# Weight sums of a hybrid encoder step: no declared VectorE time, 256 KB transfers, loaded 8 steps ahead and stored 3 behind

## The chip, the cores and the metric

The kernel runs on one core of a Trainium2 chip. The metric is the device time of one launch in microseconds. Five engines work side by side and are synchronised by semaphores: TensorE (PE; its weight loads are the row PEld), VectorE (DVE), ScalarE (ACT), GpSimd (POOL) and SyncE (SP), which issues most of the DMA transfers in the order of its queue.

## What is computed

One layer of an encoder, for a prompt of 2048 rows and for a decode batch of 8 sequences with 16 rows each, which share the weights. All is float32.

```python
h   = rms_norm(x, norm_g[0]);  z = h @ w_in          # one projection, 3592 columns
att = chunk-band attention(qa, ka, va)               # 8 heads x 64, own chunk of 64 and 8 before it
hb  = mLSTM(qb, kb, vb, ib, fb)                      # 4 heads x 128, chunked recurrence
mix = concat(rms_norm(att), sigmoid(ob) * headnorm(hb)) @ w_out
x   = x + rms_norm(mix, norm_g[1])
u   = rms_norm(x, norm_g[2]) @ w_up                  # 1024 -> 5632
y   = causal depthwise conv of width 3 over u
f   = (gelu(gate) * up) @ w_down                     # 2816 -> 1024
x   = x + rms_norm(f, norm_g[3])
```

Outputs are both groups' x, the keys and values, the mLSTM states and the convolution's tails.

## The kernel before

**Products.** Every float32 operand is split into a rounded high part (ScalarE) and a remainder (VectorE), and a product is three TensorE matmuls (`mm3`, lines 95 to 97). The FFN's two products use a scheme of seven half-size products in place of eight, which needs sums and differences of weight blocks besides the blocks themselves.

**Stages.** In the first stage `w_in` is worked through in 14 groups of columns, for each of two halves of the rows (`seq`, 28 groups): `va` and `vo` groups give rows (`group_rows`, two steps for each tile of 128 rows: 18 in the first half, 16 in the second), `qk` and `qb` groups give columns (`group_T`, 12 steps). The next group's weights are loaded and split meanwhile (`load_group`, half a group at a time). Then `project` (line 964) makes `mix @ w_out` for 17 tiles, and the FFN follows in three blocks of rows.

**Pipes and pace.** Attention and mLSTM are cut into small steps that are put between the group products. Two pipes (`Pipe`) hold them: `att_stream` takes heads from a queue as their `qk` group is done, `mem_stream` takes mLSTM heads. Each step yields what it declares: TensorE us and VectorE us. The same is yielded by every group step and by the work that rides along with it: the weight split, the norms and the weight sums. `pump(pe, dve)` (line 173) adds them up in `clock` and then steps the pipes while VectorE's clock is behind `SHARE` = 0.615 of TensorE's, with at most two tries, one for each pipe in turn; at the end it forgets what VectorE's clock is behind by more than 4.0:

```python
for _ in range(2):
    if clock[1] >= SHARE * clock[0]:
        break
    turn[0] ^= 1
    c = pipes[turn[0]].step()
    ...
clock[1] = max(clock[1], SHARE * clock[0] - (0.0 if idle == 2 else 4.0))
```

Nothing in this pace measures the chip: it sets the order of the program alone. A compile-time scheduler then places the instructions on each engine, mostly in that order; the loads that are wrapped in `keep_in_program_order` keep theirs.

**The drain.** `project` loads tiles two ahead. When it comes to tile 8 (line 970), whose rows need the second half's attention, it runs both pipes empty (`drain`, line 960) and opens the FFN's memory over that of the first stage (`open_ffn`, line 1039). From there on the pipes hold the FFN's norm and transposes (`h2_units`; x2r is loaded at line 1069, scaled at 1081, transposed at 1089).

**A step of attention.** `load_head` loads a head's query, key and value blocks (lines 339 and after). `att_unit` makes scores (lines 384, 385), adds the bias and takes the row minimum on VectorE (line 395), exponentiates on ScalarE (396), transposes (67), splits (407, 408), multiplies with the values (420, 421) and adds the halves (427). After a pair of heads the block is scaled (438, `attst`) and stored to `mixd` (442). For 640 keys the unit declares 0.533 and 0.667 us, then 0.535 and 0.667, and every second unit 1.2 and 0.34 more; a head load declares 0, about 1.8 and then 0.34 to 0.68, the scaling 0.43 and 0.7.

**The weight sums.** `weight_sums` (line 1175) makes the blocks that the seven-product scheme needs: 22 blocks of `w_up` and 11 of `w_down`, each of 128 x 2048 float32 (1 MB), seen as four pieces of 128 x 512. A block is loaded with one transfer (L1185) to the tile `wsum` (one buffer), four steps go by, four VectorE additions or subtractions (L1189) overwrite the pieces in the order of `up` or `down` in four more steps, and one transfer stores the block (L1191) to `wsd` or `wtd` in device memory. That makes 11 steps a block, 363 in all, one for each group step from the second group on (line 1251). Each addition declares 0.69 us of VectorE. The FFN stage reads `wsd` and `wtd` again as 256 KB pieces (`wu<-wsd`, `wdr<-wtd`).

Of the kernel before, what the change touches and what calls it, by code (L numbers as in the profile page):

```python
# [3 lines left out]

# [6 lines left out]
F32 = mybir.dt.float32  # L11
# [6 lines left out]
P = 128  # L18
# [26 lines left out]
def hymba_step(ctx: ExitStack, tc: tile.TileContext, I: dict, O: dict):  # L45
    nc = tc.nc
# [7 lines left out]
    def ps_mm(name):  # L54
        return psum.tile([P, 512], F32, tag="mm", name=name)

    def ps_big(name):
        return psum.tile([P, 1024], F32, tag="big", name=name)

    def ps_sm(name):  # L60
        return psum.tile([P, 512], F32, tag="sm", name=name)
# [66 lines left out]
    pr = p1.enter_context(tc.tile_pool(name="pr", bufs=1))  # L128
# [920 lines left out]
    def quad(name):  # L1049
        return ffn.p3.tile([P, 512], F32, tag="q", name=name, bufs=11)  # L1050
# [124 lines left out]
    def weight_sums():  # L1175


        add, sub = ALU.add, ALU.subtract
        up = ((2, 3, 2, add), (3, 0, 3, sub), (0, 2, 0, sub), (1, 1, 0, sub))
        down = ((0, 1, 0, sub), (1, 2, 1, sub), (2, 2, 0, sub), (3, 3, 2, sub))  # L1180
        todo = [(I["w_up"][f], wsd[f], up, f"u{f}") for f in range(NF)]
        todo += [(I["w_down"][i], wtd[i], down, f"d{i}") for i in range(NF // 2)]
        for src, dst, plan, nm in todo:
            t = pr.tile([P, 4, 512], F32, tag="wsum", name=f"wsum{nm}", bufs=1)
            tc.keep_in_program_order(nc.sync.dma_start(t, src.rearrange("p (a n) -> p a n", a=4)))  # L1185
            for _ in range(4):
                yield 0.0, 0.0
            for o, x, y, op in plan:
                nc.vector.tensor_tensor(t[:, o, :], t[:, x, :], t[:, y, :], op=op)  # L1189
                yield 0.0, 0.69  # L1190
            nc.sync.dma_start(dst.rearrange("p (a n) -> p a n", a=4), t)  # L1191
            for _ in range(3):
                yield 0.0, 0.0

    def norm_steps(half):

# [16 lines left out]
    next(norms)  # L1213
    load_bias()
    sums = weight_sums()
    for n_, (half, gi) in enumerate(seq):
        wh, wl, _ = pend
# [5 lines left out]
        i = int(g[2])  # L1223
        nm = f"{g}_{half}"
# [129 lines left out]
    def evacuate(b, j, acc, dh):  # L1354

        t = FBLOCKS[b][j]
        half = half_row(j, dh, f"fr{t}_{dh}")
        ssq = p3.tile([P, 1], F32, tag=f"dssq{j}", name=f"dssq{t}_{dh}", bufs=2)
        if b < len(FBLOCKS) - 1 or dh == 0:
            nc.vector.tensor_copy(half, acc)  # L1360
            acc = half
        nc.scalar.activation(junk, acc, AF.Square, accum_out=ssq)
        return half, acc, ssq
# [58 lines left out]
    for b, tiles in enumerate(FBLOCKS):  # L1422
        last = b == len(FBLOCKS) - 1
        nt = len(tiles)
        n = HALF[b]
# [96 lines left out]
        for f in range(NF):  # L1522
# [5 lines left out]
            nm = f"{b}_{f}"  # L1528
            a, d_, ec = ps_mm(f"ua{nm}"), ps_sm(f"ub{nm}"), ps_big(f"uec{nm}")
            e, c = ec[:, 0:512], ec[:, 512:1024]  # L1530
# [75 lines left out]
        if not last:  # L1606
# [4 lines left out]
            for q in range(42):  # L1611
                p, u = divmod(q, 6)
# [24 lines left out]
                for j in range(3):  # L1637
# [4 lines left out]
                    elif p == D2:  # L1642
                        o = quad(f"c11_{b}_{j}")
# [7 lines left out]
                    elif p == D4:  # L1651
                        o = quad(f"c21_{b}_{j}")
# [9 lines left out]
        for dh in range(2):  # L1662
# [50 lines left out]
            for j in range(nt):  # L1713
                half, _, ssq = evacuate(b, j, accs[j], dh)
# [98 lines left out]
```

## Time and profile before

| | us |
|---|---|
| median of 3 runs | 2854.73 (2854.33 to 2854.81) |
| the profiled execution | 2856.95 |
| its span, first to last instruction | 2855.2 |
| PE busy | 2722.0 |
| DVE busy | 1973.3 |
| mean granted TensorE clock | 0.986 |

The profile is one execution of the program. Busy times are those of each engine's instructions; a matmul's end is modelled, so a full PE is not PE at its peak. A row of a group gives the line, engine, operation, what is written and read, the count, and busy and mean times. In rows of waits, the instruction named first stood idle until the one behind the arrow was done. "SPq" rows are DMA issues on SP's queue; the rows of DMA issues give the size of one and the median time from issue to landing. The granted clock (PEclk) is the share of full TensorE speed. By the stretches of the span, the first stage lasts until about 1035 us, the output projection until about 1440, the FFN from there to the end.

### The profile page before, as it was taken

How to read it: one execution, taken by the hardware profiler on the slowest of the kernel's cores; microseconds unless marked ns; L12 is line 12 of the kernel's file. 1: busy time of each engine (PE TensorE's matmuls, PEld its weight loads, DVE VectorE, ACT ScalarE, POOL GpSimd, SP SyncE). 2: the span in 40 equal slices, each digit the busy share in tenths (PEclk: the TensorE clock that was granted, in tenths of full speed). 3: DMA queues.
4: the chain of work that ended last, by engine and by line, in shares of the span. 5: the costliest groups of instructions: out<-in, count | busy, mean ns of one | idle time of the engine just before them, and what ended most of it. 6: DMA issues, size and time to landing. Idle time of an engine off the chain costs nothing.

```text
span 2855.2 us, 47306 instructions
## 1 busy us (share of the span) xinstructions
PE 2722.0 (95%) x16389; PEld 2538.4 (89%) x16389; DVE 1973.3 (69%) x3640; ACT 1437.2 (50%) x2908; POOL 436.3 (15%) x876
## 2 busy tenths in 40 slices
PE   7899999989999999988999999999999999999998
PEld 7899998888889997876899998889999878999887
DVE  5355456666646667765688888858888885888855
ACT  4345444634436565463455555754545665555543
POOL 1000001111100003302411110011111121222221
PEclk9999999999999999998999999999999999999999
DMA  6654458578776665434665556765555797555586
GB/s 232 218 177 145 143 192 275 171 261 276 265 235 206 220 194 171 126 91 145 215 195 178 168 176 202 263 226 157 175 176 168 247 335 236 177 176 178 176 293 203
DMA packets 342831, 575.47 MB, mean 202 GB/s; under 512 B 57442, under 2 KB 173630, under 8 KB 334014
## 3 DMA queue, kind: packets, MB, share of 16 engines
q1 hardware_dynamic: 303998, 538.61, 58.8%
q10 hardware_dynamic: 38592, 33.83, 3.6%
q8 instruction: 129, 2.11, 0.3%
q14 instruction: 112, 0.92, 0.1%
HBM read 424.24 MB, written 151.21 MB: 202 GB/s over the span
## 4 chain that ended last, share of the span: by engine, by line
PE 51%; DMA 3%; DVE 3%; issue 2%; ACT 1%; POOL 1%; SPq 0%; DVEq 0%; POOLq 0%; ACTq 0%
PE uec L95 6%; PE uec L96 6%; PE uec L97 6%; PE ua L97 3%; PE ua L96 3%; PE ua L95 3%; PE dn L97 3%; PE dn L95 3%; PE dn L96 3%; PE dnm L97 2%; PE dnm L95 2%; PE dnm L96 2%; PE ub L96 1%; PE ub L97 1%; PE ub L95 1%
## 5 line engine op out<-in xcount | busy, mean ns | idle before, releaser
L95 PE MATMUL uec<-B,wuh 128*128 128x384 f32 (+1 forms) x720 | 234.3, 327 | 1.5 <-DVE uu L1438 1.5
L96 PE MATMUL uec<-B,wuh 128*128 128x384 f32 (+1 forms) x720 | 235.2, 327 | 0.0
L97 PE MATMUL uec<-B,wul 128*128 128x384 f32 (+1 forms) x720 | 234.2, 327 | 0.0
L1285 ACT CAST wuh<-wu 128x512 fp32r<-128x512 f32 x315 | 172.9, 617 | 81.5 <-PE uec L96 79.9
L1286 DVE TENSOR_TENSOR wul<-wu,wuh 128x512 fp32r<-128x512 f32 x315 | 202.7, 684 | 2.9 <-DMA x2d<-mx 2.9
L95 PE MATMUL dn<-wdh,gh 128*128 128x512 f32 x422 | 167.3, 396 | 11.7 <-ACT gh L1285 8.7
L96 PE MATMUL dn<-wdl,gh 128*128 128x512 f32 x422 | 167.8, 398 | 0.0
L97 PE MATMUL dn<-wdh,gl 128*128 128x512 f32 x422 | 163.5, 401 | 1.4 <-DVE gl L1286 1.4
L95 PE MATMUL vo<-wi_h,hT 128*128 128x256 f32 x544 | 156.6, 288 | 0.0
L96 PE MATMUL vo<-wi_l,hT 128*128 128x256 f32 x544 | 155.3, 286 | 0.0
L97 PE MATMUL vo<-wi_h,hT 128*128 128x256 f32 x544 | 155.2, 285 | 0.0
L1286 DVE TENSOR_TENSOR wdl<-wdr,wdh 128x512 fp32r<-128x512 f32 x198 | 127.4, 690 | 28.5 <-ACT wdh L1285 25.2
L396 ACT ACTIVATE tmp<-tmp,mn 128x640 f32<-128x640 f32 (+4 forms) x128 | 97.7, 764 | 80.6 <-DVE mn L395 73.1
L1285 ACT CAST wdh<-wdr 128x512 fp32r<-128x512 f32 x198 | 112.1, 618 | 50.1 <-DMA wdr<-in_w_down 21.6
L95 PEld LDWEIGHTS uec<-B,wuh 128*128 128x128 f32 x720 | 135.0, 188 | 2.7 <-DVE uu L1438 2.5
L96 PEld LDWEIGHTS uec<-B,wuh 128*128 128x128 f32 x720 | 135.2, 188 | 0.1
L97 PEld LDWEIGHTS uec<-B,wul 128*128 128x128 f32 x720 | 135.1, 188 | 0.0
L395 DVE CUSTOM_DVE_ANT_0 tmp<-s,nb 128x640 f32<-128x640 f32 (+4 forms) x128 | 94.0, 735 | 56.2 <-PE s L385 51.6
L95 PE MATMUL qk<-hT,wi_h 128*128 128x384 f32 (+1 forms) x384 | 129.0, 336 | 1.5 <-ACT qk_st L228 0.9
L96 PE MATMUL qk<-hT,wi_h 128*128 128x384 f32 (+1 forms) x384 | 129.0, 336 | 0.0
L97 PE MATMUL qk<-hT,wi_l 128*128 128x384 f32 (+1 forms) x384 | 128.9, 336 | 0.0
L95 PE MATMUL qb<-hT,wi_h 128*128 128x384 f32 (+1 forms) x384 | 127.9, 333 | 0.5 <-ACT qb_st L226 0.5
(428 smaller groups left out, 8898.0 us busy)
## 6 DMA issues: line engine op xcount, KB each, us to landing
wu<-wsd SPq DMA_DIRECT2D x264, 256.0 KB, 3.6
wu<-in_w_up SPq DMA_DIRECT2D x198, 256.0 KB, 3.8
wdr<-in_w_down SPq DMA_DIRECT2D x110, 256.0 KB, 5.7
wi_raw<-in_w_in SPq DMA_DIRECT2D x52, 512.0 KB, 4.8
gq<-gsd SPq DMA_DIRECT2D x62, 384.0 KB, 5.0
wsumu<-in_w_up SPq DMA_DIRECT2D x22, 1024.0 KB, 7.1
wsd<-wsumu SPq DMA_DIRECT2D x22, 1024.0 KB, 5.5
wdr<-wtd SPq DMA_DIRECT2D x88, 256.0 KB, 5.6
```

The source lines that it names most:

```text
L95: nc.tensor.matmul(out, ah, bh, start=start, stop=False, skip_group_check=onto)
L96: nc.tensor.matmul(out, ah, bl, start=False, stop=False, skip_group_check=onto)
L97: nc.tensor.matmul(out, al, bh, start=False, stop=stop, skip_group_check=onto)
L395: nc.vector.tensor_tensor_reduce(o_, s_, b_, 1.0, 3e38, ALU.add, ALU.min, accum_out=mn)
L396: nc.scalar.activation(tmp[:, :n], tmp[:, :n], AF.Exp, bias=mn, scale=-1.0, accum_out=rsum[:, i % 4, hh:hh + 1])
L1285: nc.scalar.copy(h, r)
L1286: nc.vector.tensor_tensor(l, r, h, op=ALU.subtract)
```

## The change

Each block is now four tiles of 128 x 512 (tags `wsum0` to `wsum3`, two buffers each, so 16 KB instead of 8 KB of each partition). A table `acts` gives what is done at which step. With n the block's number: piece i is loaded at step 11n + i, addition e is made at step 11n + 11 + e, and the piece that it wrote is stored at step 11n + 14 + e. So the first addition comes eight steps after the last piece's load, and each store three steps after its addition. Within one step the earlier block's actions come first. The loads keep their place in the program order, as before. All steps yield 0.0, 0.0, the additions too. There are still 132 additions of 128 x 512, and a block still takes 11 steps; the last store is at step 369. The 33 loads and 33 stores of 1 MB become 132 loads and 132 stores of 256 KB, whose rows of 2 KB lie 8 KB apart in device memory.

```diff
-from collections import deque
+from collections import defaultdict, deque
...
         todo += [(I["w_down"][i], wtd[i], down, f"d{i}") for i in range(NF // 2)]
-        for src, dst, plan, nm in todo:
-            t = pr.tile([P, 4, 512], F32, tag="wsum", name=f"wsum{nm}", bufs=1)
-            tc.keep_in_program_order(nc.sync.dma_start(t, src.rearrange("p (a n) -> p a n", a=4)))
-            for _ in range(4):
-                yield 0.0, 0.0
-            for o, x, y, op in plan:
-                nc.vector.tensor_tensor(t[:, o, :], t[:, x, :], t[:, y, :], op=op)
-                yield 0.0, 0.69
-            nc.sync.dma_start(dst.rearrange("p (a n) -> p a n", a=4), t)
-            for _ in range(3):
-                yield 0.0, 0.0
+        acts = defaultdict(list)
+        for n, (src, dst, plan, nm) in enumerate(todo):
+            t = []
+
+            def load(i, src=src, t=t, nm=nm):
+                t.append(pr.tile([P, 512], F32, tag=f"wsum{i}", name=f"wsum{nm}_{i}", bufs=2))
+                tc.keep_in_program_order(nc.sync.dma_start(t[i], src[:, i * 512:(i + 1) * 512]))
+
+            def combine(e, plan=plan, t=t):
+                o, x, y, op = plan[e]
+                nc.vector.tensor_tensor(t[o], t[x], t[y], op=op)
+
+            def store(e, dst=dst, plan=plan, t=t):
+                o = plan[e][0]
+                nc.sync.dma_start(dst[:, o * 512:(o + 1) * 512], t[o])
+
+            for i in range(4):
+                acts[11 * n + i].append(lambda i=i, f=load: f(i))
+                acts[11 * n + 11 + i].append(lambda i=i, f=combine: f(i))
+                acts[11 * n + 14 + i].append(lambda i=i, f=store: f(i))
+        for step in range(max(acts) + 1):
+            for act in acts[step]:
+                act()
+            yield 0.0, 0.0
```

## The prediction

> **What bounds the kernel now.** I read the page first, then the busy time by stretch, then instructions and waits of the stretches where TensorE is not full.
>
> ```profile
> span 2855.2 us, 47306 instructions
> ...
> PE 2722.0 (95%) x16389; PEld 2538.4 (89%) x16389; DVE 1973.3 (69%) x3640; ACT 1437.2 (50%) x2908; POOL 436.3 (15%) x876
> ```
>
> TensorE is the bound: 133 us of the span are not covered by its matmuls, and no change outside TensorE can win more than that, plus what slow clock costs. So the question is where those 133 us lie and which of them the weight sums can reach. By stretch (the first columns after the length are busy us and instruction counts of PE, PEld, DVE, ACT and POOL, then granted clock, DMA share, GB/s):
>
> ```profile
> core 0: us, PE busy (x) PEld busy (x) DVE busy (x) ACT busy (x) POOL busy (x), PEclk, DMA share, GB/s
> 206.00:386.00 180.00, 180.00 (x1295) 179.16 (x1294) 86.57 (x185) 87.86 (x199) 1.70 (x11) 1.00 0.45 138
> 386.00:505.00 119.00, 108.67 (x742) 102.46 (x741) 75.50 (x193) 55.74 (x149) 14.09 (x39) 1.00 0.83 265
> ...
> 600.00:710.00 110.00, 102.60 (x701) 97.67 (x700) 62.11 (x178) 43.13 (x118) 16.55 (x47) 0.98 0.82 274
> 710.00:826.00 116.00, 106.12 (x653) 96.79 (x652) 64.89 (x174) 45.25 (x113) 19.80 (x45) 0.96 0.74 245
> 826.00:1035.00 209.00, 205.77 (x1560) 202.62 (x1560) 125.55 (x291) 112.93 (x284) 11.94 (x38) 1.00 0.70 222
> ...
> 1240.00:1296.00 56.00, 42.52 (x257) 35.50 (x255) 35.15 (x72) 33.85 (x69) 0.73 (x2) 0.88 0.21 58
> 1296.00:1308.00 12.00, 11.99 (x53) 9.14 (x52) 3.00 (x5) 1.10 (x3) 0.19 (x1) 1.00 0.44 100
> 1308.00:1328.00 20.00, 7.76 (x33) 6.59 (x34) 14.16 (x12) 8.36 (x16) 12.38 (x14) 0.60 0.54 187
> ```
>
> Two stretches stand out. From 1240 to 1296 TensorE idles 13.48 us and runs at a clock of 0.88; from 1308 to 1328 it idles 12.24 us at 0.60. The first is the drain: `load(8)` (line 970) empties both pipes before the FFN's memory is opened, and whatever attention is left runs alone, with no product between its steps:
>
> ```profile
> L395 DVE CUSTOM_DVE_ANT_0 tmp<-s,nb x16: 814/824/825, 1239.4 to 1287.5; 128x640 f32<-128x640 f32 x16
> ```
>
> So 16 score units are left over. The second hole is its echo:
>
> ```profile
> 1302.43 0.69 DVE L438 TENSOR_TENSOR attst<-ao,rinv 128x512 f32<-128x512 f32 x1 [4.79 <-PE ao L67]
> ...
> 1303.15 0.55 SPq L442 DMA_DIRECT2D mixd<-attst  x1
> ...
> 1304.41 0.94 SPq L1069 DMA_DIRECT2D x2r<-x2d  x2
> ...
> 1313.71 1.11 PE L1089 MATMUL h2T_pt<-ident,x2r 128*128 128x128 f32 x4 [5.72 <-DVE x2r L1081]
> ...
> 1318.67 1.97 PE L67 MATMUL mT_pt<-ident,mr 128*128 128x128 f32 x8 [0.71 <-DVE mr L987]
> 1325.26 1.97 PE L67 MATMUL mT_pt<-ident,mr 128*128 128x128 f32 x8 [4.62 <-DVE mr L987]
> ```
>
> SP issues in order: the store of the last attention block waits for L438, and behind it stand the loads of x2r that the first FFN transposes need. They go out at 1304.41 and the transpose starts 9.3 us later.
>
> **Part 1: the sums declare no time.** Each `pump` steps the pipes until declared VectorE time reaches 0.615 of declared TensorE time, at most two tries, one for each pipe. A block of sums now declares 4 x 0.69 us over its 11 steps. The second half's groups take 16 (row groups) or 12 (column groups) steps. 33 blocks are 363 steps; the first half uses 5 x 18 + 8 x 12 = 186, so 177 fall in the second half: 177 x 4/11 x 0.69 = 44.4 us of declared VectorE time that will go to attention and mLSTM steps instead. What does the drain need? From the costs in the code, a pair of 640-column units declares 3.01 us VectorE and 3.34 us TensorE, net of the share 3.01 - 0.615 x 3.34 = 0.96; eight pairs 7.7. Three head loads at about 2.1 make 6.4, closings (0.70 - 0.615 x 0.43 = 0.44) 1.5: together about 16 us. Attention is tried once a pump, so in the groups where it already steps every pump freed time is dropped again (the pace forgets all but 4 us). Counting the groups from qb1 to qb3 of the second half alone, where the code as it stands leaves many pumps without a step, 12 + 16 + 12 + 16 + 12 = 68 steps free 68 x 4/11 x 0.69 = 17.1 us. That is just enough without the earlier groups, so I take the drain to be empty.
>
> Its price: idle 13.48 plus slow clock 42.52 x 0.12 = 5.10, and in the echo 12.24 plus 7.76 x 0.40 = 3.10, in all 33.9 us. The work itself does not vanish; it moves between group products, where TensorE is paid for it at full clock. The echo goes because the last `mixd` store is long past: x2r is loaded when the FFN opens, its 9.3 us lie beside the 48 output products of the row from 1296 to 1308 (11.99 us busy). Late next are the two waits on mr (0.71 and 4.62), which belong to the output projection's own norm; I leave their 5.3 us. Gain: 33.9 - 5.3 = 28.6 us. If the 11.99 us of cover were gone, 9.3 us of it would come back.
>
> How much of the clock term to count is in doubt:
>
> ```profile
> PE ot L420 <- ACT pth L407: 7.9, 7, 2.2
> ...
> 1276.00:1278.00 2.00, 0.46 (x4) 0.19 (x2) 0.00 (x0) 1.59 (x5) 0.72 (x2) 1.00 0.44 178
> ...
> 1280.00:1282.00 2.00, 2.00 (x12) 2.00 (x11) 0.00 (x1) 0.28 (x2) 0.00 (x0) 0.50 0.00 0
> ```
>
> The clock halves right behind the longest wait, 2.2 us, so I tie the loss to the waits. The Trainium skill ("TensorE: Matmul & The Clock Gate", section What's actually happening) wants a whole idle window of about 3.4 us before the clock drops; by that rule the 5.10 us are not the drain's and the gain would be 23.5 us. The row of this case decides for the larger one.
>
> The moved steps make 826 to 1035 denser. Today it idles 3.23 us of 209. A stretch with an attention step in every pump, 206 to 386, idles nothing; 600 to 826, with the decode batch's attention among the steps, idles 17.28 of 226, which over 209 us is 16.0. So the cost is between 0 and 12.8 us; I take 5, nearer to the plain attention stretch.
>
> **Part 2: loaded 8 steps ahead, stored 3 behind.** Today VectorE runs into the load:
>
> ```profile
> L1189 DVE TENSOR_TENSOR wsumu<-wsumu x88: 668/691/891, 44.2 to 710.2; 128x512 f32<-128x512 f32 x88
> L1185 SPq DMA_DIRECT2D wsumu<-in_w_up x22: 328/424/1163, 36.0 to 698.6; - x22
> L1191 SPq DMA_DIRECT2D wsd<-wsumu x22: 320/332/612, 47.1 to 710.9; - x22
> ...
> L1191 SPq DMA_DIRECT2D wtd<-wsumd x11: 319/332/459, 729.7 to 1005.9; - x11
> ...
>   DMA wsumu<-in_w_up: 52.4, 18
> ...
>   DMA wsumd<-in_w_down: 19.2, 9
> ...
> wsumu<-in_w_up SPq DMA_DIRECT2D x22, 1024.0 KB, 7.1
> wsd<-wsumu SPq DMA_DIRECT2D x22, 1024.0 KB, 5.5
> ```
>
> 71.6 us of VectorE standing still, with everything behind in its queue. A step declares at least 1.28 us of TensorE, so 8 steps are over 10 us; the 1 MB loads land in 7.1 us. These waits go. What they cost TensorE is less:
>
> ```profile
> 44.22 2.87 DVE L1189 TENSOR_TENSOR wsumu<-wsumu 128x512 f32<-128x512 f32 x4 [4.33 <-DMA wsumu<-in_w_up]
> ...
> 49.26 1.12 PE L67 MATMUL hT_pt<-ident,xr 128*128 128x128 f32 x4 [4.19 <-DVE xr L221]
> ...
> 408.77 2.15 DVE L1189 TENSOR_TENSOR wsumu<-wsumu 128x512 f32<-128x512 f32 x3 [4.92 <-DMA wsumu<-in_w_up]
> ...
> 411.58 0.50 PE L96 MATMUL sot<-svl,sph 128*128 128x512 f32 x1 [2.10 <-DVE svl L904]
> ```
>
> Twice a norm or a decode split stood behind the waiting sums and TensorE behind that: 4.19 + 2.10 = 6.3 us, which I take. Bounds: 0, if another wait ends last, and 19, three times these two; that would be two thirds of what TensorE idles from 386 to 505 and from 600 to 826 (10.33 + 7.40 + 9.88 = 27.6 us), where many of the sums lie.
>
> **Part 3: 256 KB pieces.** The 132 additions stay, at the same 691 ns. 66 transfers become 264, 198 more issues at 0.33 to 0.42 us: 65 to 83 us of SP's queue, spread over the 970 us from 36.0 to 1005.9. SP is not on TensorE's path as long as the loads behind come early.
>
> ```profile
> SPq L339 <- DMA wsumu<-in_w_up: 6.6, 2, 3.5
> ...
> wu<-in_w_up SPq DMA_DIRECT2D x198, 256.0 KB, 3.8
> ...
> 1450.00:1700.00 250.00, 250.00 (x1437) 250.00 (x1436) 215.04 (x329) 127.93 (x206) 32.25 (x68) 1.00 0.55 174
> ```
>
> Pieces of this size already carry the FFN stage: from 1450 to 1700 the engines are 0.55 busy for 174 GB/s, 0.0032 per GB/s; with the 1 MB blocks in 386 to 505 it is 0.83 for 265, 0.0031. The same bytes cost the same. The Trainium skill ("DMA: Bandwidth & Descriptors", section Bandwidth) says to batch to 1 MiB or more, against this change; by its fit of 2.0 us plus bytes at 436 GB/s, an estimate, 264 pieces would hold a serial queue 686 us instead of 290 for the blocks. The two rows above speak against it. Value 0. To the good at most the 6.6 us for which a query load (L339) was held by a block's load, as far as TensorE saw them; to the bad as much, if two of the extra issues hold a load as long. With two buffers a load no longer waits for the store just before it.
>
> **Sum.** -28.6 - 6.3 + 5 + 0 = -29.9 us. The profiled execution took 2856.95 us (span 2855.2 and 1.75 around it) and would take 2827.0; it lies 2.2 us above the median, so on the median 2854.73 this is 2824.8, say 2825.
>
> **The rivals.** *Half the drain stays.* If mLSTM steps take two fifths of the freed 17.1 us, 10.3 of 16 us reach attention, 0.6 of the drain goes: 0.6 x (13.48 + 5.10) = 11.1, the echo stays whole because the last store is still late: -11.1 - 6.3 + 5 gives 2842. For it: one try per pump and pipe. Against: the earlier groups' 27 us, of which some must count.
>
> *More than forecast.* The denser stretch costs nothing, as 206 to 386, and the sums' waits are worth 19: 2855 - 28.6 - 19 = 2807.
>
> *Nothing moves.* The compile-time scheduler places instructions by readiness, and the freed time is forgotten; only the waits go or not: 2848 to 2855, no change.
>
> *Slower: the stores hold SP.*
>
> ```profile
> SPq L1191 <- DMA wsumu<-in_w_up: 19.5, 3, 7.3
> ...
> SPq L1191 <- DVE wsumd L1189: 14.0, 6, 3.8
> ...
> SPq L1191 <- DMA wsumd<-in_w_down: 5.7, 2, 3.7
> ```
>
> Today 33 stores hold SP 39.2 us, 1.2 us each, with weight and attention loads queued behind. If 132 stores each wait as long, SP stands 157 us, 118 more. Should a third reach TensorE, 39 us: 2854.7 - 28.6 + 39 = 2865. It decides from a share of 24% (28.6/118). For it: a store whose sum has slipped blocks the queue. Against: three steps are nearly 4 us of declared TensorE time, while today's store is issued one step behind its last sum.
>
> **How the numbers follow.** Forecast 0.58, more 0.09, half 0.17, nothing moves 0.08, slower 0.08. About 0.2%, 5.7 us, is what a measurement of this kernel can tell from no change. Faster: 0.58 + 0.09 + 0.17 = 0.84; same 0.08; slower 0.08. The range runs from 2803 (the rival of more, with 4 us of part 3's good side) to 2848 (half the drain, with part 3's bad side); it leaves out 0.16 and part of the edges. Forecast and rivals of the same sign share it, so it is one range.
>
> **What would show it.** Right: no L395 after about 1240 of the new order, the two stretches of half clock gone, x2r loads not behind an attention store; more L395 between 826 and 1035 with TensorE idle there under 10 us; no wait of L1189's successor on a load. Half: some 6 score units with idle TensorE before the FFN opens and the echo still over 10 us. Slower: SP waits on the store line above 100 us and TensorE waits for weight or attention loads between 36 and 1035. I am wrong if the drain is empty and TensorE's idle before 1035 has grown by more than 20 us, or if the drain is as long as before.

## The result, and the profile after

| | us |
|---|---|
| before, median of 4 runs | 2854.77 (2854.33 to 2855.28) |
| after, median of 4 runs | 2872.74 (2869.23 to 2875.38) |
| ratio after / before | 1.0063, 95% interval 1.0047 to 1.0079 |
| the profiled execution after | 2870.22, span 2868.5 |

The kernel became 18 us slower; the forecast was 2825 us, faster. The page of the kernel after has the same instructions on TensorE and nearly the same busy time:

```profile
span 2868.5 us, 47580 instructions
...
PE 2726.6 (95%) x16389; PEld 2540.8 (89%) x16389; DVE 1977.6 (69%) x3640; ACT 1439.0 (50%) x2908; POOL 436.3 (15%) x876
```

To see where the time went, the span is cut at the same work in both kernels: the end of the last `va` product, the first and the last `wo` product (the output projection), the end. The columns are those of the prediction's second fence. Before:

```profile
0.00:699.80 699.80, 645.45 (x4508) 625.38 (x4509) 385.60 (x920) 318.85 (x753) 64.47 (x187) 0.99 0.65 208
699.80:1068.40 368.60, 354.48 (x2540) 340.79 (x2538) 218.51 (x523) 184.99 (x459) 34.79 (x92) 0.99 0.70 226
1068.40:1414.90 346.50, 312.39 (x1659) 260.51 (x1660) 229.87 (x387) 168.17 (x395) 99.53 (x142) 0.95 0.46 142
1414.90:2855.20 1440.30, 1409.70 (x7686) 1311.74 (x7685) 1139.36 (x1813) 765.24 (x1302) 237.52 (x455) 0.99 0.64 207
```

After:

```profile
0.00:699.20 699.20, 644.27 (x4484) 623.91 (x4485) 374.02 (x893) 315.48 (x741) 57.09 (x180) 0.98 0.65 197
699.20:1092.90 393.70, 370.31 (x2637) 352.62 (x2636) 240.87 (x557) 201.44 (x490) 33.51 (x95) 0.99 0.74 226
1092.90:1425.70 332.80, 300.39 (x1587) 250.39 (x1587) 220.66 (x379) 157.25 (x376) 105.07 (x146) 0.95 0.47 153
1425.70:2868.50 1442.80, 1411.62 (x7687) 1313.91 (x7685) 1142.04 (x1813) 764.81 (x1302) 240.65 (x455) 0.99 0.64 206
```

The output projection is 13.7 us shorter and has 72 fewer matmuls: attention did move ahead of it. But the stretch before it is 25.1 us longer, 15.8 of it more busy time (97 matmuls more, 72 of them from the projection) and 9.3 more idle (393.7 - 370.3 against 368.6 - 354.5), and the FFN is 2.5 longer. The first 699 us gained nothing, although the loads of all 22 `w_up` blocks fall there in the kernel before. The two profiled executions differ by 13.3 us of span, 4.7 less than the medians do.

The drain is about half gone, the echo is there as before. The rows of score units from 1240 on, three stretches, and SP's and TensorE's rows at the opening of the FFN, all after:

```profile
L395 DVE CUSTOM_DVE_ANT_0 tmp<-s,nb x9: 802/818/825, 1243.5 to 1286.6; 128x640 f32<-128x640 f32 x9
```

```profile
1240.00:1296.00 56.00, 50.01 (x307) 42.32 (x306) 39.78 (x86) 30.54 (x75) 11.37 (x17) 1.00 0.26 82
1296.00:1308.00 12.00, 9.99 (x44) 7.68 (x43) 2.08 (x4) 1.45 (x4) 0.19 (x1) 1.00 0.45 121
1308.00:1332.00 24.00, 13.39 (x55) 10.89 (x56) 18.01 (x16) 11.64 (x21) 13.99 (x18) 0.64 0.61 195
```

```profile
1301.15 0.56 SPq L442 DMA_DIRECT2D mixd<-attst  x1
1301.77 1.05 SPq L1046 DMA_DIRECT2D g<-in_norm_g  x1
1302.86 0.92 SPq L1069 DMA_DIRECT2D x2r<-x2d  x2
```

```profile
1312.07 1.11 PE L1089 MATMUL h2T_pt<-ident,x2r 128*128 128x128 f32 x4 [6.07 <-DVE x2r L1081]
...
1323.63 1.97 PE L67 MATMUL mT_pt<-ident,mr 128*128 128x128 f32 x8 [4.62 <-DVE mr L987]
```

16 score units behind 1240 became 9, the idle time from 1240 to 1296 fell from 13.48 to 5.99 us and the clock there rose from 0.88 to 1.00. The hole behind it has the same chain, rows and waits as before.

And VectorE still stands and waits for the sums' loads. VectorE's waits, then the issues of the pieces on SP, after:

```profile
DVE wsumu L1193 <- DMA wsumu<-in_w_up: 60.0, 26, 7.7
DVE wsumd L1193 <- DMA wsumd<-in_w_down: 13.4, 8, 3.4
```

```profile
L1189 SPq DMA_DIRECT2D wsumu<-in_w_up x88: 327/432/1973, 34.6 to 809.8; - x88
L1197 SPq DMA_DIRECT2D wsd<-wsumu x88: 319/348/1281, 92.4 to 816.5; - x88
```

73.4 us, against 71.6 before. Eight steps of the program are not eight steps of the chip: by the rows of both lines, the last of a block's four loads is issued 4.9 us (median) ahead of its first addition, where the 1 MB load was issued 7.1 us ahead; only the first piece is early, 24.1 us. A piece takes 5.2 us to land (4.9 for `w_down`), so the addition still meets the load.

### The profile page after: what moved, and what is told of

Read it like the earlier page. It is cut to its first block, busy times and chain, and to the rows that moved or that the text cites. A ratio compares the mean times of both kernels' runs of the same rounds, so it can differ in the third digit from the quotient of the medians.

```text
span 2868.5 us, 47580 instructions
## 1 busy us (share of the span) xinstructions
PE 2726.6 (95%) x16389; PEld 2540.8 (89%) x16389; DVE 1977.6 (69%) x3640; ACT 1439.0 (50%) x2908; POOL 436.3 (15%) x876
## 4 chain that ended last, share of the span: by engine, by line
PE 49%; DVE 3%; DMA 3%; issue 2%; ACT 1%; POOL 1%; SPq 0%; DVEq 0%; ACTq 0%; POOLq 0%
PE uec L95 6%; PE uec L96 6%; PE uec L97 6%; PE ua L97 3%; PE ua L96 3%; PE ua L95 3%; PE dn L95 3%; PE dn L97 3%; PE dn L96 3%; PE dnm L97 2%; PE dnm L95 2%; PE dnm L96 2%; PE ub L96 1%; PE ub L97 1%; PE ub L95 1%
## 5 line engine op out<-in xcount | busy, mean ns | idle before, releaser
L408 DVE TENSOR_TENSOR ptl<-pt,pth 128x640 fp32r<-128x640 f32 (+4 forms) x128 | 93.4, 736 | 68.3 <-ACT pth L407 67.6
```

The source lines that it names most:

```text
L408: nc.vector.tensor_tensor(s.ptl[:, sl, qc], ptv, s.pth[:, sl, qc], op=ALU.subtract)
```

## The experiments

The times of the kernel before differ a little from one group of runs to the next (medians 2850.94, 2854.35, 2855.42, 2854.58 and 2856.46 us), so each run is given as its ratio to the kernel before in its own group, with the 95% interval. 0.0035 is 10 us.

The theories at the start: A, the pace costs, because attention moved between the group products waits there as long as it did in the drain; B, the transfers cost, and the pace by itself gains. From the fifth run on: C, it is the number of issues in SP's queue; D, the cut into runs of 2 KB; E, each transfer by itself, whichever queue issues it.

### One edit at a time

**e1_pace**, the pace alone, on the kernel before:

```diff
-                yield 0.0, 0.69
+                yield 0.0, 0.0
```

> The kernel before with one change: each addition of the sums declares 0.0 us of VectorE time instead of 0.69; blocks, steps and transfers stay. Theory A (the pace costs: attention moved between the group products waits there for its own chain as long as it did in the drain): near the changed kernel, 2862 to 2878 us, with under 5 us of TensorE idle from 1240 to 1296 and at least 8 us more idle than before ahead of the output projection. Theory B (the transfers cost, the pace alone gains what the drain cost): 2832 to 2848 us. The place of the units in the compiled order: 24 of 64 score units behind the first output product, 28 in the changed kernel, 34 before.

Measured: 2834.55 us, 0.9941 (0.9927 to 0.9955). Theory B: the pace alone makes the kernel faster.

**e2_moves**, the change without the pace, on the kernel after:

```diff
-            yield 0.0, 0.0
+            yield 0.0, 0.69 if 0 <= (step - 11) % 11 < 4 <= step else 0.0
```

> The changed kernel with one change: each addition declares 0.69 us again; the 256 KB pieces, the lead of 8 steps and the stores 3 steps behind stay. Theory A (the pace costs): as before, 2850 to 2860 us, the drain as long as before (16 score units). Theory B (the transfers cost): 2865 to 2885 us, drain as before, and the additional idle of TensorE lies ahead of the output projection.

Measured: 2871.34 us, 1.0070 (1.0051 to 1.0088). Theory B again; its stretch from 1240 to 1296 holds 16 score units, as before. One part of B missed: in its profiled execution (2861.19 us) TensorE's idle ahead of the output projection is 69.4 us, 68.5 before, and 9.1 us more lie in the projection itself.

**e3_1mb**, the kernel after with whole blocks (the comments here and under f1 and f2 are not in the code):

```diff
+            acts[11 * n + 3].append(load)       # t [P, 4, 512], bufs=2, one 1 MB load
             for i in range(4):
-                acts[11 * n + i].append(lambda i=i, f=load: f(i))
                 acts[11 * n + 11 + i].append(lambda i=i, f=combine: f(i))
-                acts[11 * n + 14 + i].append(lambda i=i, f=store: f(i))
+            acts[11 * n + 17].append(store)     # one 1 MB store
```

> The changed kernel (zero declared, load 8 steps ahead, store 3 steps behind) with one 1 MB load and one 1 MB store a block instead of four of 256 KB each. If the number of pieces costs (198 more issues on SP): 2845 to 2862 us, under the changed kernel's 2872.7 by more than 10. If not: 2866 to 2878 us. VectorE's wait for the loads: under 30 us if the lead works in blocks, 60 to 80 if the compiled order sets it.

Measured: 2811.28 us, 0.9857 (0.9839 to 0.9876), well below both kernels and below what either theory gave. With the pieces 40 us of gain became 18 of loss. VectorE waits 55.1 us for the loads, in neither of the ranges. Besides the number of transfers one thing differs: the first three pieces were loaded, and stored, one to three steps earlier than the block. This is the best version of the study.

**e4_pieces**, the kernel before with four loads together and four stores together:

```diff
-            tc.keep_in_program_order(nc.sync.dma_start(t, src.rearrange("p (a n) -> p a n", a=4)))
+            for i in range(4):
+                tc.keep_in_program_order(nc.sync.dma_start(t[i], src[:, i * 512:(i + 1) * 512]))
...
-            nc.sync.dma_start(dst.rearrange("p (a n) -> p a n", a=4), t)
+            for o, _, _, _ in plan:
+                nc.sync.dma_start(dst[:, o * 512:(o + 1) * 512], t[o])
```

> The kernel before with one change: each block moves as four loads and four stores of 256 KB at the old steps (loads together 5 steps ahead of the first addition, stores together one step behind the last), 0.69 us declared. If the pieces cost by their number: 2860 to 2872 us. If not: 2850 to 2858 us. VectorE's wait for the loads: 50 to 75 us, as before, if the pieces land together with the block.

Measured: 2866.58 us, 1.0051 (1.0035 to 1.0068): the pieces cost time here too, 15 us. VectorE waits 75.7 us for the loads.

Two later runs fill the corners that were missing. **h2_lead** is e3_1mb with the `yield` line of e2_moves:

> The 1 MB version with 0.69 us declared for each addition, so only the lead of 8 steps and the stores 3 steps behind differ from the kernel before. If the edits add up (pace alone 0.994, pace with lead 0.986): 0.989 to 0.994. If the lead is worth something only together with the pace: 0.997 to 1.003.

Measured: 2845.19 us, 0.9967 (0.9950 to 0.9985). The lead alone gains a little; with the pace it gains more. **i1_corner** is e4_pieces with the `yield` line of e1_pace:

> The kernel before with pieces of 256 KB at the old steps and zero declared: pace and pieces without the lead. Pace alone gave 0.994. If the pieces cost what they cost in the kernel before (0.005): 0.997 to 1.002. If the pace makes SyncE's queue fuller and the pieces dearer, as with the lead (0.021): 1.008 to 1.018.

Measured: 2849.13 us, 0.9980 (0.9966 to 0.9994): at the old steps the pieces cost 0.004 over the pace alone, little. All eight corners:

| | 1 MB blocks | 256 KB pieces | price of the pieces |
|---|---|---|---|
| old steps, 0.69 declared | 1 | 1.0051 | 0.0051 (15 us) |
| old steps, 0 declared | 0.9941 | 0.9980 | 0.0039 (11 us) |
| lead, 0.69 declared | 0.9967 | 1.0070 | 0.0103 (29 us) |
| lead, 0 declared | 0.9857 | 1.0063 | 0.0206 (59 us) |

In every row the pieces lose; pace and lead each win with blocks. The lead, which wins 0.003 and 0.008 with blocks, loses 0.002 and 0.008 with pieces. f4_shift below shows that another order of the same work can be worth 0.005, so the smaller of these numbers are read for their sign at most.

### What of a piece costs

These runs start from e3_1mb (lead, zero declared). **f1_loads** and **f2_stores** cut one side only:

```diff
-            acts[11 * n + 3].append(load)
+            for i in range(4):                  # f1: t[0][:, i, :] <- src[:, i * 512:(i + 1) * 512]
+                acts[11 * n + i].append(lambda i=i, f=load: f(i))
...
-            acts[11 * n + 17].append(store)
+            for i in range(4):                  # f2: dst[:, o * 512:(o + 1) * 512] <- t[0][:, o, :]
+                acts[11 * n + 14 + i].append(lambda i=i, f=store: f(i))
```

> Declares zero, loads 8 steps ahead, stores 3 behind; four loads of 256 KB a block (one a step, as in the changed kernel) and one store of 1 MB. The version with 1 MB both ways took 2811.3 us at a ratio of 0.986, the changed kernel with 256 KB both ways 1.006. If the small loads carry the cost: ratio 0.998 to 1.010. If the small stores carry it: 0.982 to 0.992. If both share it: 0.993 to 0.998.

> As the last, with one load of 1 MB a block and four stores of 256 KB, each 3 steps behind its sum. If the small stores carry the cost: ratio 0.998 to 1.010. If the small loads do: 0.982 to 0.992. If both share it: 0.993 to 0.998.

Measured: f1 0.9961 (0.9944 to 0.9978), f2 0.9957 (0.9942 to 0.9973). Each side carries half, 0.0104 and 0.0100 over e3_1mb, and they add up to the 0.0206. So the cost needs no store that waits for its sum: loads wait for no sum and cost the same. Nor does it need the fixed place in the program order: the added loads have it and the added stores do not.

**f3_rows** cuts the block by rows:

```diff
+                r = slice(32 * i, 32 * i + 32)  # load and store of t[0][r]: 32 partitions x 8 KB
```

> Declares zero, the same lead; each block in four loads and four stores of 256 KB, but cut by rows (32 partitions of 8 KB each) instead of by columns (128 partitions of 2 KB each). So 264 issues as in the changed kernel and contiguous runs of 8 KB as with 1 MB. Theory C (the number of issues and of their waits on SyncE's queue costs): ratio 1.000 to 1.010, as the changed kernel. Theory D (the cut into runs of 2 KB costs on the DMA engines): 0.982 to 0.990, as with 1 MB.

Measured: 1.0173 (1.0149 to 1.0198), above theory C's range too. Theory D falls: with runs of 8 KB, as in the whole block, four transfers cost even more than pieces with runs of 2 KB, 0.0316 over e3_1mb against 0.0206. Why the cut by rows is dearer was not taken apart; its issues take SP longer, as the table under g2_tiny shows. VectorE waits less for the sums' loads here than in e3_1mb (55.1 us), and yet the kernel is 0.03 slower:

```profile
DVE wsumu L1195 <- DMA wsumu<-in_w_up: 25.7, 11, 4.4
DVE wsumd L1195 <- DMA wsumd<-in_w_down: 15.1, 6, 5.6
```

So it is not VectorE's waits for the sums' loads that set the time.

**f4_shift**, the control, loads at step 11n + 1 and stores at 11n + 19:

> A control: 1 MB both ways and zero declared, the load 10 instead of 8 steps ahead and the store 5 instead of 3 behind. If the gain of the 1 MB version belongs to the scheme: ratio 0.982 to 0.990. If it is an accident of one compiled order: anywhere from 0.990 to 1.010.

Measured: 0.9908 (0.9884 to 0.9932), partly in the one range and partly in the other. The scheme gains in another order too, but a shift that should mean nothing is worth 0.005. A difference of that size between two runs of this study shows nothing by itself. Measured from f4_shift instead of e3_1mb, the price of the pieces is 0.0155 (44 us) instead of 0.0206 (59 us), and f1's and f2's is 0.005, no longer clear of the shift.

**h3_512**, halves of 512 KB (loads at steps 11n + 1 and 11n + 3, both stores at 11n + 17):

> The 1 MB version with each block in two loads and two stores of 512 KB: 66 issues more than with 1 MB, a third of the changed kernel's 198. If the cost goes with the number of issues: 0.986 plus a third of 0.0206, 0.990 to 0.996. If it sets in only with pieces of 256 KB: 0.983 to 0.989.

Measured: 0.9902 (0.9880 to 0.9923): 66 issues more than in e3_1mb come with 0.0045, 99 (f1, f2) with 0.010, 198 (the kernel after) with 0.0206. The price grows with the number, but 0.0045 is the size of f4's shift, and the interval reaches into both ranges: whether 66 cost anything is not shown.

### The queue

**g2_tiny** adds transfers of 64 B to e3_1mb, which nothing depends on:

```diff
+            def tiny(i, nm=nm):
+                tc.keep_in_program_order(nc.sync.dma_start(dt_([1, 16], f"tiny{nm}_{i}"), I["norm_g"][0:1, 0:16]))
+
+            for i in range(6):
+                acts[11 * n + (0, 1, 2, 14, 15, 16)[i]].append(lambda i=i, f=tiny: f(i))
```

> The 1 MB version (ratio 0.986) with 6 transfers of 64 B a block added on SyncE, from one DRAM tensor to another, at the steps at which the changed kernel has its extra loads and stores: 198 more issues, 264 in all, that nobody waits for and that wait for no sum. If the bare number of issues costs: 0.998 to 1.010. If it is what the pieces wait for in the queue (a sum, a buffer): 0.984 to 0.992. This work is not in the reference and changes no output.

Measured: 2886.70 us, 1.0123 (1.0099 to 1.0147), 0.0266 over e3_1mb, or 76 us. The added issues on SP in this run (smallest, median and longest in ns):

```profile
L1204 SPq DMA_DIRECT2D tinyu<-in_norm_g x132: 488/524/1684, 34.8 to 856.7; - x132
L1204 SPq DMA_DIRECT2D tinyd<-in_norm_g x66: 488/539/1197, 677.7 to 1156.9; - x66
```

13 KB in all, no sum to wait for, and it costs more than the pieces: 198 x 0.53 = 105 us of SP's time. The next table sets all DMA issues on SP, summed over the profiled execution, against what the cut, or here the small transfers, added to the time:

| | SP's issues, us | more, us | price, us |
|---|---|---|---|
| old steps, 0.69 declared: before, e4_pieces | 768, 839 | 71 | 15 |
| old steps, 0 declared: e1_pace, i1_corner | 781, 838 | 56 | 11 |
| lead, 0.69 declared: h2_lead, e2_moves | 768, 845 | 77 | 29 |
| lead, 0 declared: e3_1mb, f1_loads | 774, 820 | 46 | 30 |
| lead, 0 declared: e3_1mb, f2_stores | 774, 800 | 26 | 29 |
| lead, 0 declared: e3_1mb, the kernel after | 774, 857 | 83 | 59 |
| lead, 0 declared: e3_1mb, g2_tiny | 774, 902 | 128 | 76 |
| lead, 0 declared: e3_1mb, f3_rows | 774, 911 | 137 | 90 |

With lead and no declared time the price is 0.6 to 0.7 of the time added on SP (in f2_stores all of it), whatever the transfers hold. At the old steps only a fifth comes out. So an issue's time has no fixed price; and since the issues themselves can take longer (a load of the sums up to 1973 ns in the kernel after, up to 888 in e3_1mb), the table does not say which of the two comes first.

**g1_pool** and **g4_pool1mb** take the sums' transfers off SP, the first in the kernel after, the second in e3_1mb:

```diff
-                tc.keep_in_program_order(nc.sync.dma_start(t[i], src[:, i * 512:(i + 1) * 512]))
+                tc.keep_in_program_order(nc.gpsimd.dma_start(t[i], src[:, i * 512:(i + 1) * 512]))
...
-                nc.sync.dma_start(dst[:, o * 512:(o + 1) * 512], t[o])
+                nc.gpsimd.dma_start(dst[:, o * 512:(o + 1) * 512], t[o])
```

> The changed kernel with the sums' 132 loads and 132 stores of 256 KB issued on GpSimd's queue (busy 15% of the span) instead of SyncE's. Theory C (they cost because they stand in SyncE's queue, in order with the weight and attention loads): ratio 0.978 to 0.992, as with 1 MB blocks. Theory E (each transfer costs by itself, whichever queue issues it): 1.000 to 1.010, as the changed kernel.

> The 1 MB version with the sums' 33 loads and 33 stores issued on GpSimd's queue. Theory C, if SyncE's queue still costs time with 66 transfers in it: 0.972 to 0.982. If 66 cost nothing: 0.984 to 0.990. Theory E: as with SyncE, 0.984 to 0.990.

Measured: pieces 0.9987 (0.9974 to 1.0001), blocks 0.9971 (0.9957 to 0.9985). Both miss what theories C and E gave: with blocks, GpSimd's queue is 0.011 slower than SP's. Read as a pair they speak against theory E, that a transfer costs wherever it is issued: on GpSimd's queue the pieces cost 0.0016, with an interval of about 0.002 to either side, on SP's 0.0206. The same 264 transfers with the same bytes hardly cost anything once they do not stand in SP's order. One doubt stays: stores on GpSimd's queue hold it until their sums are done, 130 us in all with blocks and 98 with pieces in the view of GpSimd's waits from 12 to 1100 us, and that could hide a part of a price of the pieces.

**i2_act**, the kernel after with only the 132 stores on ScalarE's queue (`nc.scalar.dma_start`):

> The changed kernel with the 132 stores of 256 KB issued on ScalarE's queue (SyncE keeps the 132 loads: 66 more than with 1 MB both ways). Theory C: what 66 more issues cost with pieces of 512 KB, ratio 0.988 to 0.996, if ScalarE loses nothing. Theory E (each transfer costs, whichever queue): 1.000 to 1.010. Stores that wait for their sum on ScalarE could also hold its roundings: above 1.010.

Measured: 0.9998 (0.9982 to 1.0013), 0.0065 below the kernel after, at the edge of E's range and outside C's. By the price of e3_1mb, 132 issues fewer on SP should give 0.0137; half of it is there. Whether ScalarE's queue has a price as well this run does not show.

### Two tries that went wrong

**h1_merge** (on e3_1mb) and **h4_merge0** (on the kernel before) were to test the price the other way, by 88 issues fewer:

```diff
-        for r in range(2):
-            nc.sync.dma_start(qr[r * 64:r * 64 + 64, :], qTd[pair][kg][rows, :])
+        twice = lambda a: bass.AP(a.tensor, a.offset, [[0, 2], *a.ap])
+        nc.sync.dma_start(qr, twice(qTd[pair][kg][rows, :]))
```

(and the same for the keys)

> The 1 MB version (ratio 0.986) with each pair of query or key loads of a head (twice the same 64 rows of 128 KB) issued as one transfer of 256 KB: 88 issues fewer on SyncE, the same bytes. At what an extra issue cost in the pieces, 58 us over 198 or 0.29 us, 88 fewer are worth 26 us: ratio 0.973 to 0.982. If only the sums' own transfers disturb the order: 0.983 to 0.990.

> The kernel before with the same merged query and key loads, 88 issues fewer on SyncE, nothing else. At the price that the pieces had there (1.005, 15 us for 198 issues, 0.07 us each): 0.996 to 1.000. At 0.29 us each: 0.986 to 0.994. If a load of twice the size holds back more than its issue saves: above 1.000.

Measured: 1.0651 (1.0631 to 1.0670) and 1.0802 (1.0784 to 1.0820), slower by far. ScalarE's wait for the key loads, before and in h4_merge0:

```profile
  DMA kraw<-kTd: 19.2, 9
```

```profile
  DMA kraw<-kTd: 105.6, 21
```

From the end of an issue to the rounding of the keys the shortest time is 2.2 us before and 7.4 in h4_merge0 (7.3 in h1_merge). The merged transfer itself lands late, so these runs say nothing on the number of issues; that fewer issues than in e3_1mb gain more stays untested. A rule of the Trainium skill ("DMA: Bandwidth & Descriptors", section Why a DMA increments its semaphore by 16 and not by 1) would explain it: a transfer runs on the largest number of engines, up to 16, that divides the outermost dimension of both its sides; that is 2 for the merged one (2 and 128) and 16 for each half (64 and 64). The slow landing agrees; no run shows how many engines worked.

**g3_echo**, e3_1mb with the attention stores on ScalarE's queue:

```diff
-        nc.sync.dma_start(mixd[kg][:, :, pair * P:(pair + 1) * P], st)
+        nc.scalar.dma_start(mixd[kg][:, :, pair * P:(pair + 1) * P], st)
```

> The 1 MB version with the stores of the attention blocks (L442) issued on ScalarE's queue, so that the FFN's first loads of x2r no longer stand behind the last of them. If that store holds the loads: the idle stretch at the opening of the FFN goes from about 12 us to under 6, ratio 0.976 to 0.983. If the loads are late for another reason, or the stores now hold ScalarE: 0.984 to 0.992 and the stretch stays.

Measured: 0.9892 (0.9871 to 0.9914), no gain on 0.9857. Its loads of x2r go out at 1246.08, ahead of the last attention store, and the hole is still there; ScalarE's rows up to the first of that norm, and TensorE's:

```profile
1259.13 0.63 ACT L1018 ACTIVATE mt<-mx 128x512 fp32r<-128x512 f32 x1 [4.29 <-DVE mx L1016]
...
1259.76 1.04 ACT L1077 ACTIVATE sq<-x2r 128x1024 f32<-128x1024 f32 x1
```

```profile
1263.17 1.11 PE L1089 MATMUL h2T_pt<-ident,x2r 128*128 128x128 f32 x4 [4.87 <-DVE x2r L1081]
...
1268.16 1.97 PE L67 MATMUL mT_pt<-ident,mr 128*128 128x128 f32 x8 [0.71 <-DVE mr L987]
1274.75 1.97 PE L67 MATMUL mT_pt<-ident,mr 128*128 128x128 f32 x8 [4.62 <-DVE mr L987]
```

The square of x2r (L1077) starts 13.7 us after the load was issued, right behind L1018, the output projection's own norm, which stands ahead of it on ScalarE and waits for L1016, the copy of the last `wo` product. The same pair in the kernel before:

```profile
1308.82 0.63 ACT L1018 ACTIVATE mt<-mx 128x512 fp32r<-128x512 f32 x1 [4.28 <-DVE mx L1016]
...
1310.29 1.06 ACT L1077 ACTIVATE sq<-x2r 128x1024 f32<-128x1024 f32 x1 [0.75 <-DMA x2r<-x2d]
```

There the load held the square by 0.75 us only. So in ScalarE's order the FFN's first norm comes behind the row of output products and does not lie beside it, even where x2r is loaded early.

## Why the prediction was wrong

The step that failed is part 3: "198 more issues at 0.33 to 0.42 us: 65 to 83 us of SP's queue", "SP is not on TensorE's path", value 0, at worst 6.6 us. The number of issues was right, and so was their time on SP (83 us more in the kernel after than in e3_1mb). The value was not: beside the other two edits the pieces cost 59 us (44 against the order of f4_shift). With the lead and no declared time it is shown that more transfers in SP's queue cost this, and that neither bytes nor waits for sums are needed for it: transfers of 64 B that wait for no sum cost as much (g2), cut loads and cut stores cost about half each (f1, f2), and on GpSimd's queue hardly any difference between pieces and blocks is left (g1 with g4). The runs of 2 KB are not the reason either, for a cut into larger runs is dearer still (f3); that it is dearer shows that the number is not all, and the time that SP spends issuing fits better.

How the cost reaches TensorE stays open. Where it lies is seen in the profile, in the same stages of e3_1mb:

```profile
0.00:665.70 665.70, 633.03 (x4496) 617.82 (x4497) 379.01 (x897) 316.25 (x745) 55.73 (x183) 0.99 0.64 208
665.70:1049.50 383.80, 366.67 (x2630) 353.09 (x2628) 240.32 (x563) 202.08 (x491) 34.77 (x96) 0.98 0.72 235
1049.50:1372.10 322.60, 296.91 (x1582) 249.52 (x1583) 217.57 (x369) 154.04 (x372) 100.18 (x142) 0.95 0.47 154
1372.10:2814.90 1442.80, 1410.82 (x7686) 1312.48 (x7684) 1140.55 (x1813) 764.49 (x1302) 242.58 (x455) 0.99 0.63 206
```

33.5, 9.9 and 10.2 us lie in the three stages ahead of the FFN and nothing in it: 35.2 of them are idle time of TensorE (110.7 against 75.5 over the three), the other 18.4 longer matmuls (the clock of the first stage is 0.98 against 0.99). No single wait explains it. Among the kernels with lead and no declared time, ScalarE's waiting for transfers grows, summed over the view of its waits from 12 to 1100 us: 202 us in e3_1mb, 226 in f4_shift, 231 in f2_stores, 252 in f1_loads, 273 in the kernel after, 300 in g2_tiny, 304 in f3_rows, in the order of their times (h3_512, with 245, is out of it). Outside this family it does not hold: it is 277 us in the kernel before, more than in the slower kernel after, and 243 in e4_pieces, which is slower still than the kernel before. So this sum is a trace of the cost at most. One row of it, ScalarE's waits for query loads, 12 to 1100 us, after and in e3_1mb:

```profile
ACT qs L344 <- DMA qraw<-qTd: 23.1, 7, 10.1
```

```profile
ACT qs L344 <- DMA qraw<-qTd: 9.5, 4, 4.0
```

SP issues in order. Its 378 us of issuing between 12 and 1060 us are 36% of 1048, which looks idle, but an issue put between two others can move all that stand behind it, the loads of the next operands among them; this is argued, no run tests it by itself. "As long as the loads behind come early" was the condition, and I did not test it against the rows: ScalarE's waits for loads were in the trace of before.

Two more things stay open. Why the pieces cost 0.004 to 0.005 at the old steps, where four stand together, and 0.010 to 0.021 with the lead, where they stand one a step, is not told apart: no run has the lead and four together. And any difference of about 0.005 can be the compiled order's own (f4).

Point by point:

- *Part 1, the pace.* Right in sign and near in size: alone it gives 0.0059, 17 us, where -28.6 + 5 = 23.6 were forecast. Score units behind the first `wo` product fall from 34 to 24:

```profile
L395 DVE CUSTOM_DVE_ANT_0 tmp<-s,nb x24: 806/816/825, 1082.0 to 1249.9; 128x640 f32<-128x640 f32 x24
```

  In the kernel after they fall to 28 only. Of the 28.6, the drain's part was largely right in e1_pace, whose last 56 us ahead of the FFN's opening idle 3.3 us at full clock:

```profile
1200.00:1256.00 56.00, 52.69 (x308) 44.24 (x307) 38.32 (x81) 27.99 (x71) 13.21 (x20) 1.00 0.28 86
```

  The choice on the clock fits: in the kernel after, where the longest wait from 1240 to 1296 is 1.95 us, the clock there stays at 1.00. The echo's 10.0 (12.24 + 3.10 - 5.3) was wrong. The late attention store, which I took for the cause of the hole, can have held the square of x2r by 0.75 us at most before; what failed is "its 9.3 us lie beside the 48 output products", which ScalarE's order does not let happen (g3). The hole is there in e1_pace, e3_1mb, g3_echo and the kernel after alike. The price of the denser stretch, 5, was too small where the pace stands alone: TensorE's idle between the last `va` and the first `wo` product is 10.4 us longer in e1_pace and 9.3 in the kernel after, but 3.0 in e3_1mb.
- *Part 2, the lead.* "These waits go" was wrong: 73.4 us instead of 71.6, because the last load of a block goes out just ahead of its addition (4.9 us), whatever the program's steps say; whether the compiled order or SP's waits put it there is not told apart. That VectorE's waits for sums hardly matter was nearer the truth than I allowed: f3 has fewer than e3_1mb. The lead has its worth all the same, with blocks 0.003 alone and 0.008 beside the pace (0.003 in the order of f4_shift), 9 and 24 us where 6.3 were forecast; only the 24 are clear of another order's 0.005, and through what, the runs do not say.
- *Parts 1 and 2 together* are e3_1mb: 0.0143, 41 us, where 29.9 were forecast; in the order of f4_shift 0.0092, 26 us. Without the pieces the sign would have been right. That the sum comes this near is partly luck: the drain's gain was nearly there, the echo's was not, and the lead gave more than its reason explains.
- *The rivals.* The rival of the other sign named the right queue and the wrong mechanism: at the line of the stores SP waits 84.0 us after and 71.1 before, 12.9 more and not 118 (the prediction's 39.2 were the three longest rows for sums and loads alone), and g2 and f1 show that the loss needs no waiting store. The Trainium skill's rule ("DMA: Bandwidth & Descriptors", section Bandwidth: batch to 1 MiB or more) spoke against the change and the outcome agrees with it; I set it aside by rows of throughput, and throughput was not the question. By its figures, measured on GpSimd's queue, size is what counts, and here 64 B transfers cost as much. Another sentence of that page (section Issuing engines are not separate DMA queues) calls the sequencer's time to start a transfer "usually small relative to the DMA itself". It is so here, 0.43 us (median) against 5.2 us to landing for a piece of `w_up`, and the added transfers cost all the same, so small against the transfer does not mean free.
- *What would show it.* The two conditions under which I called myself wrong did not come: the drain was half there, and idle time ahead of the output projection grew by 9.9 us (78.3 against 68.5), not by 20. The signs of the rival *half the drain stays* came, 9 score units and 10.6 us of idle in the stretch of the echo, with a time of the other sign. I had no sign ready for a loss spread over every stream.

## What to carry over

Count the issues that a change adds to an in-order queue that other loads share, and give their time a price between nothing and the whole of it: here a fifth of it came out at the old steps, and more than half with lead and pace. The queue's share of busy time does not show which. Splitting transfers needs a queue of its own or a gain above the issues' time, and a cut into pieces is measured apart from edits that win. A lead written in program steps is worth what is left of it on the chip: read it from the issue row and the row of the first use. And before a load is blamed for a late start, look at what stands ahead of its first user on that engine.

## What the runs showed of the hardware

- A transfer of 64 B from device memory to device memory holds SP's queue for 524 to 539 ns (medians, g2), longer than one of 256 KB between device memory and the core's own, 348 to 432 ns (the kernel after).
- One transfer that reads 64 rows twice into 128 partitions was used 7.3 us (h1) and 7.4 us (h4) after its issue at the earliest, the two halves as two transfers 2.2 us (before).
- The sums' 1 MB transfers made the kernel 0.011 slower on GpSimd's queue than on SP's (g4 against e3; 0.006 against f4).
- Per GB/s the DMA engines were busy a little longer with pieces: between the last `va` and the first `wo` product 0.74 for 226 GB/s, 0.0033, against 0.72 for 235, 0.0031, with blocks. "The same bytes cost the same" was 7% off.
- TensorE's granted clock halves without a long wait: in the kernel after it goes to 0.50 at 1098.49 us, and in the 3.41 us ahead of that TensorE was busy 1.71 us and no wait was longer than 1.11 us. In the kernel before, at 1278.03 us, it was busy 1.50 of them. So it did not take the whole idle window that the prediction weighed against its row.
